# Two attention layers of a four-layer transformer trunk rewritten: masks without matmuls, transposes per key block, wider products

## The chip, the cores and the metric

The kernel runs on one core of a Trainium2 chip. The metric is the time of one execution on the device in microseconds; the profile is of one such execution. TensorE (PE) multiplies, VectorE (DVE), ScalarE (ACT) and GpSimd (POOL) do the rest, and SP and POOL also issue the DMAs.

## The reference

Input x is 512 rows of 1024 numbers in float32. Four residual layers follow each other, each with an RMS norm ahead: stick-breaking attention (16 heads of 64), a SwiGLU FFN (2816 wide), differential attention (8 heads, each with two maps of 64 and values of 128), and a second FFN.

```python
# stick-breaking, per head and block of 128 queries
earlier = key_pos[None, :] < q_pos[:, None]
log_keep = where(earlier, log_sigmoid(-z), 0.0)
log_after = cumsum(log_keep, reverse=True) - log_keep
weight = where(earlier, exp(log_sigmoid(z) + log_after), 0.0)
out = weight @ v
# differential: keys of the same or an earlier chunk of 64 are visible
q, k = rms_norm(q, q_g), rms_norm(k, k_g)     # per 64, then partial rotary
a = softmax(where(visible, q1 @ k1.T * scale, -1e30)) \
    - lam * softmax(where(visible, q2 @ k2.T * scale, -1e30))
o = rms_norm(a @ v, sub_g) * (1 - lam_init)
# FFN
x = x + (silu(h @ w_gate) * (h @ w_up)) @ w_down
```

## The kernel before

Activations lie transposed, as eight tiles of 128 features by 512 rows. Every float32 product is made of three matmuls of rounded halves (`mm3`, lines 203 to 205): high by high, high by low, low by high. Weights come in units of 128 x 1024. In the FFNs `wload` (L111 to L113) fetches a unit on SP's queue and splits it on ACT and DVE; in the attention layers `wload_dma` (L121 to L123) fetches it on POOL's queue into `whi`, ACT writes its negative into `wlo`, and a second DMA on POOL's queue adds the unit to that. Two sets of four buffers hold the halves.

An attention layer works pair by pair. In layer 0, q and k of a pair of heads are products of 512 columns (`ps_q`, `ps_k`), in layer 1 they are made for two heads at a time with 256 columns (`ps_nat`, `qk_chunk`, four `qk_nat` buffers), normalised per 64 columns and rotated there, the last two partly on POOL, and then transposed (`tqk`, L661). `stack_q` and `stack_k` lay the halves of q and k one above the other, so that one product of depth 128 gives two of the three terms: ACT and DVE write four pieces of 64 x 512, and two DMAs on POOL's queue copy k's into the other half (L278).

Scores (`scores`, L284 to L286) of one block of 128 queries are two products with a mask matmul between them, which adds -1e30 to the masked part of the diagonal block through an identity. Layer 0 takes two sigmoids of them, DVE runs a scan (L403) and DVE or, for every other block, POOL multiplies (L412). Layer 1 takes the maximum (L678), exps with their sums (L679), scales on POOL (L688) and combines on DVE (L692). A head is worked in two halves of two query blocks (`attend`), each with its transposes (`wt_group`, L296 to L304), the split into `wt_hi` and `wt_lo` (L306, L307) and value products of 256 columns into `av`. In layer 1 `head_out` then transposes the head's result (`tn`), takes its square sum, normalises (L731), transposes back (`tb`) and splits it (L743, L744). `out_proj` multiplies by the output weights (`ps_o`).

The pools of layer 1 hold eight PSUM banks of 512 columns: two for `ps_nat`, two for scores, one each for `tqk`, `tp`, `tn` and `av`. The program is written head by head, and a scheduler of the build sets the order on each engine from it by dependences and buffers; on the chip each engine then works in exactly that order. In the program of layer 1 the stacks of the next pair stand between the two halves of the odd head, and the q, k and v products of the next pair in the even and the odd head.

## Time and profile before

| | |
|---|---|
| median of 3 runs | 1323.24 us (1320.13 to 1327.58) |
| the profiled execution | 1320.52 us, span 1318.7 us |
| PE busy | 1258.5 us (95%), 6598 matmul records |
| DVE, ACT, POOL busy | 686.6, 539.5, 201.2 us |
| DMA | 149.16 MB |
| mean granted clock of PE | 0.985 |

Busy PE time is the time with at least one matmul under way; matmuls overlap, so the distance from start to start tells what one costs. Stages by the first and last matmul: layer 0 to 295.6 us, first FFN to 666.5, layer 1 to 954.5, second FFN to the end.

### The profile page before, as it was taken

How to read it: one execution, taken by the hardware profiler on the slowest of the kernel's cores; microseconds unless marked ns; L12 is line 12 of the kernel's file. 1: busy time of each engine (PE TensorE's matmuls, PEld its weight loads, DVE VectorE, ACT ScalarE, POOL GpSimd, SP SyncE). 2: the span in 40 equal slices, each digit the busy share in tenths (PEclk: the TensorE clock that was granted, in tenths of full speed). 3: DMA queues.
4: the chain of work that ended last, by engine and by line, in shares of the span. 5: the costliest groups of instructions: out<-in, count | busy, mean ns of one | idle time of the engine just before them, and what ended most of it. 6: DMA issues, size and time to landing. Idle time of an engine off the chain costs nothing.

```text
span 1318.7 us, 16917 instructions
## 1 busy us (share of the span) xinstructions
PE 1258.5 (95%) x6598; PEld 1066.8 (81%) x6598; DVE 686.6 (52%) x1250; ACT 539.5 (41%) x896; POOL 201.2 (15%) x283
## 2 busy tenths in 40 slices
PE   7999989889999999999989999988899999999998
PEld 5887878777888888888889999967688888888887
DVE  5465656655543344344533777875654434443442
ACT  5566655554331222122334666653443212221220
POOL 2233333310000000000015635531000000000000
PEclk9999999999999999999989999998999999999999
DMA  7656465353333333332368677553433333333222
GB/s 233 153 122 154 111 142 112 76 125 109 96 96 96 96 96 96 96 96 89 103 146 183 142 154 143 131 106 68 114 96 96 96 96 96 96 98 96 95 87 89
DMA packets 46159, 149.16 MB, mean 113 GB/s; under 512 B 6400, under 2 KB 6400, under 8 KB 46080
## 3 DMA queue, kind: packets, MB, share of 16 engines
q0 software_dynamic: 22464, 73.41, 25.7%
q1 hardware_dynamic: 23472, 74.67, 18.0%
q8 instruction: 52, 0.85, 0.3%
q14 instruction: 27, 0.22, 0.1%
q10 hardware_dynamic: 144, 0.01, 0.0%
HBM read 137.58 MB, written 2.10 MB: 106 GB/s over the span
## 4 chain that ended last, share of the span: by engine, by line
PE 74%; DMA 8%; issue 7%; DVE 5%; POOL 3%; ACT 2%; SPq 0%; POOLq 0%; DVEq 0%; ACTq 0%
PE ps_d L203 6%; PE ps_d L205 6%; PE ps_u L204 6%; PE ps_u L203 6%; PE ps_u L205 6%; PE ps_d L204 6%; PE ps_g L204 6%; PE ps_g L205 6%; PE ps_g L203 6%; PE ps_nat L203 2%; PE ps_nat L204 2%; PE ps_nat L205 2%; DMA whi<-in_wv 2%; DMA wlo<-in_wo 2%; DMA whi<-in_wqk 1%
## 5 line engine op out<-in xcount | busy, mean ns | idle before, releaser
L112 ACT ACTIVATE whi<-wraw 128x1024 fp32r<-128x1024 f32 (+1 forms) x138 | 142.7, 1037 | 475.1 <-PE ps_d L204 148.6
L113 DVE TENSOR_TENSOR wlo<-wraw,whi 128x1024 fp32r<-128x1024 f32 (+1 forms) x138 | 164.2, 1192 | 38.4 <-ACT whi L112 30.1
L204 PE MATMUL ps_nat<-wlo,hhi 128*128 128x256 f32 x512 | 148.3, 290 | 3.5 <-DMA wlo<-in_wqk 3.5
L203 PE MATMUL ps_nat<-whi,hhi 128*128 128x256 f32 x512 | 149.0, 291 | 2.6 <-issue 1.7
L205 PE MATMUL ps_nat<-whi,hlo 128*128 128x256 f32 x512 | 147.9, 289 | 0.0
L203 PE MATMUL ps_d<-ahi,whi 128*128 128x512 f32 x352 | 138.0, 394 | 0.0
L203 PE MATMUL ps_g<-hhi,whi 128*128 128x512 f32 x352 | 137.9, 392 | 0.0
L205 PE MATMUL ps_d<-ahi,wlo 128*128 128x512 f32 x352 | 137.7, 392 | 0.0
L205 PE MATMUL ps_g<-hhi,wlo 128*128 128x512 f32 x352 | 137.2, 390 | 0.0
L204 PE MATMUL ps_g<-hlo,whi 128*128 128x512 f32 x352 | 136.9, 390 | 0.0
L205 PE MATMUL ps_u<-hhi,wlo 128*128 128x512 f32 x352 | 136.9, 389 | 0.0
L204 PE MATMUL ps_u<-hlo,whi 128*128 128x512 f32 x352 | 136.9, 389 | 0.0
L203 PE MATMUL ps_u<-hhi,whi 128*128 128x512 f32 x352 | 136.9, 389 | 0.0
L204 PE MATMUL ps_d<-alo,whi 128*128 128x512 f32 x352 | 136.3, 388 | 0.0
L203 PEld LDWEIGHTS ps_nat<-whi,hhi 128*128 128x128 f32 x512 | 100.4, 196 | 4.6 <-issue 1.8
L204 PEld LDWEIGHTS ps_nat<-wlo,hhi 128*128 128x128 f32 x512 | 100.3, 196 | 4.6 <-DMA wlo<-in_wqk 4.2
L495 DVE TENSOR_TENSOR x<-x,ps_d 128x512 f32<-128x512 f32 x48 | 32.8, 687 | 132.5 <-PE ps_d L205 132.5
L205 PEld LDWEIGHTS ps_nat<-whi,hlo 128*128 128x128 f32 x512 | 100.2, 196 | 0.2
L483 DVE TENSOR_TENSOR u<-ps_u,rbc 128x512 f32<-128x512 f32 x44 | 30.4, 690 | 132.7 <-PE ps_u L205 132.7
L122 ACT ACTIVATE wlo<-whi 128x1024 fp32r<-128x1024 f32 x62 | 65.5, 1059 | 82.8 <-DMA whi<-in_wqk 29.0
L205 PEld LDWEIGHTS ps_d<-ahi,wlo 128*128 128x128 f32 x352 | 66.1, 188 | 15.4
L204 PEld LDWEIGHTS ps_d<-alo,whi 128*128 128x128 f32 x352 | 66.1, 188 | 14.8
(211 smaller groups left out, 2509.7 us busy)
## 6 DMA issues: line engine op xcount, KB each, us to landing
wraw<-in_wgu SPq DMA_DIRECT2D x88, 512.0 KB, 3.5
wraw<-in_wd SPq DMA_DIRECT2D x32, 512.0 KB, 3.5
whi<-in_wqk POOLq DMA_DIRECT2D x30, 512.0 KB, 4.1
wlo<-in_wqk POOLq DMA_DIRECT2D x30, 512.0 KB, 5.7
whi<-in_wv POOLq DMA_DIRECT2D x16, 512.0 KB, 5.8
wlo<-in_wv POOLq DMA_DIRECT2D x16, 512.0 KB, 5.7
k<-k POOLq DMA_DIRECT2D x32, 256.0 KB, 3.8
whi<-in_wo POOLq DMA_DIRECT2D x16, 512.0 KB, 4.5
```

The costliest lines, as they stand in the source:

```text
L112: A.activation(hi[:, :cols], raw[:, :cols], AF.Copy)
L113: eng.tensor_tensor(lo[:, :cols], raw[:, :cols], hi.bitcast(F32)[:, :cols], op=ALU.subtract)
L122: A.activation(lo, hi.bitcast(F32), AF.Copy, scale=-1.0)
L203: T.matmul(ps, lh[0], rh[0], start=first, stop=False)
L204: T.matmul(ps, lh[0], rh[1], start=False, stop=False)
L205: T.matmul(ps, lh[1], rh[0], start=False, stop=last)
L483: V.tensor_tensor(u32, pu, norm.bc, op=ALU.mult)
L495: V.tensor_tensor(x[m], x[m], ps, op=ALU.add)
```

## The change

The FFN code keeps its products; only their first four gate and up units per layer are loaded by `wload_dma`, and the unsplit units have a pool of three. Weights have five buffers for each half instead of four.

- Masks: no mask matmuls. In layer 0 the scan multiplies and adds an identity block (`delta`) from an initial 0, so that everything at and behind the diagonal becomes 0. In layer 1 DVE writes the masked corner of 64 x 64 of both maps into the scores.
- A head as a whole: blocks 3, 2, 1, 0 are weighed one after the other, the transposes are gathered by key block into banks for blocks (2, 3), (1) and (0), and the value products have 512, 384, 256 and 256 columns.
- Stacks: ACT and DVE write one pair of 128 x 512 halves (`hl`, one buffer), and eight DMAs on SP's queue lay them out: four for q, four for k.
- Layer 1: q and k of two heads come from one product of 512 columns, with two `qk_nat` buffers of twice the size; scores of both maps share one tile of two banks (one buffer); the gains are folded into the q stack and the rotation tables, which run on DVE; 1/s moves into `head_out`, whose squares come from four ACT instructions with accumulator. The stack transposes, `tn` and `tb` share one bank (`tq`). The stacks of the next pair follow `head_out` of the odd head.
- POOL issues DMAs only.

```diff
+WB = 5
...
+    def halves(pool, src, gain=None):
+        hl = pool.tile([P, 2, S], F32R, tag="hl", bufs=1, name="hl")
+        if gain is None:
+            A.activation(hl[:, 0], src, AF.Copy)
+            V.tensor_tensor(hl[:, 1], src, hl.bitcast(F32)[:, 0], op=ALU.subtract)
+        else:
+            A.activation(hl[:, 0], src, AF.Copy, scale=gain)
+            V.scalar_tensor_tensor(
+                hl[:, 1], src, gain, hl.bitcast(F32)[:, 0], op0=ALU.mult, op1=ALU.subtract
+            )
+        return hl
+
+    def stack_q(pool, src, gain=None):
+        hl = halves(pool, src, gain)
         q2 = pool.tile([P, 2, S], F32R, tag="q2", name="q2")
         for e in range(2):
             r = slice(e * 64, e * 64 + 64)
             o = slice(64 - e * 64, 128 - e * 64)
-            A.activation(q2[r, e], src[r], AF.Copy)
-            V.tensor_tensor(q2[o, e], src[r], q2.bitcast(F32)[r, e], op=ALU.subtract)
+            nc.sync.dma_start(out=q2.bitcast(F32)[r, e], in_=hl.bitcast(F32)[r, 0])
+            nc.sync.dma_start(out=q2.bitcast(F32)[o, e], in_=hl.bitcast(F32)[r, 1])
         return q2
 
-    def stack_k(pool, src):
+    def stack_k(pool, src, gain=None):
+        hl = halves(pool, src, gain)
         k2 = pool.tile([P, 2, 2, S], F32R, tag="k2", name="k2")
         for e in range(2):
             r = slice(e * 64, e * 64 + 64)
             o = slice(64 - e * 64, 128 - e * 64)
-            A.activation(k2[r, 0, e], src[r], AF.Copy)
-            V.tensor_tensor(
-                k2[r, 1, e], src[r], k2.bitcast(F32)[r, 0, e], op=ALU.subtract
-            )
-            G.dma_start(out=k2[o, :, e], in_=k2[r, :, e])
+            nc.sync.dma_start(out=k2.bitcast(F32)[r, :, e], in_=hl.bitcast(F32)[r])
+            nc.sync.dma_start(out=k2.bitcast(F32)[o, :, e], in_=hl.bitcast(F32)[r])
         return k2
...
+    def wt_bank(tpp, wts, w, kts):
+        tp = tpp.tile([P, S], F32, tag="tp", name="tp")
+        b = WOFF[kts[0]]
+        for kt in kts:
+            for qt in range(TT - 1, kt - 1, -1):
+                o = WOFF[kt] - b + (TT - 1 - qt) * P
+                T.transpose(tp[:, o : o + P], w[qt][:, kt * P : (kt + 1) * P], ident)
+        r = slice(b, WOFF[kts[-1] + 1])
+        n = r.stop - r.start
+        A.activation(wts[0][:, r], tp[:, :n], AF.Copy)
+        V.tensor_tensor(
+            wts[1][:, r], tp[:, :n], wts[0].bitcast(F32)[:, r], op=ALU.subtract
+        )
+
+    def wt_chunk(wts, kt):
+        n = S - kt * P if kt < 3 else 256
+        r = slice(WOFF[kt], WOFF[kt] + n)
+        return n, wts[0][:, r], wts[1][:, r]
+
+    def attend(tpp, wts, weigh):
+        w = [None] * TT
+        for qt in (3, 2):
+            w[qt] = weigh(qt)
+        wt_bank(tpp, wts, w, (2, 3))
+        w[1] = weigh(1)
+        wt_bank(tpp, wts, w, (1,))
+        w[0] = weigh(0)
+        wt_bank(tpp, wts, w, (0,))
...
-                scores(ps, q2, k2, e, qt, mask_sb)
+                scores(ps, q2, k2, e, qt)
...
-                    ones[:, 0:1].to_broadcast([P, n]),
-                    1.0,
+                    delta[:, S - n :][:, ::-1],
+                    0.0,
                     ALU.mult,
-                    ALU.mult,
-                )
-                eng = G if qt % 2 == 1 else V
-                eng.tensor_tensor(w[:, : n - 1], w[:, : n - 1], qq[:, 1:n], op=ALU.mult)
+                    ALU.add,
+                )
+                V.tensor_tensor(w[:, :n], w[:, :n], qq[:, 1:], op=ALU.mult)
...
-            qp = st.enter_context(tc.tile_pool(name="qp1", bufs=4))
+            qp = st.enter_context(tc.tile_pool(name="qp1", bufs=2))
...
-            scp = st.enter_context(tc.tile_pool(name="sc1", bufs=2, space=PSUM))
-            tpp = st.enter_context(tc.tile_pool(name="tp1", bufs=1, space=PSUM))
+            scp = st.enter_context(tc.tile_pool(name="sc1", bufs=1, space=PSUM))
+            tpp = st.enter_context(tc.tile_pool(name="tp1", bufs=2, space=PSUM))
+            tqp = st.enter_context(tc.tile_pool(name="tq1", bufs=1, space=PSUM))
...
+                gemm_nat([wqk1[c, j] for j in range(4)], h, evac, 512)
...
+                ps = scp.tile([P, 2, S], F32, tag="sc", name="sc")
+                for e in range(2):
+                    scores(ps[:, e], q2, k2, e, qt)
+                V.memset(ps[0:64, :, n - 64 : n], NEG)
+                V.reduce_max(nm, ps[:, :, :n], axis=AX.X, negate=True)
...
+            def head_out(av, ss):
+                ot = at.tile([P, S], F32, tag="ho", name="ot")
+                A.activation(ot, av, AF.Copy)
+                rs = sm.tile([P, TT], F32, tag="rs1", name="rs1")
+                V.reciprocal(rs, ss[:, 0])
+                tp = tqp.tile([P, S], F32, tag="tq", name="tn")
+                for t in range(TT):
+                    o = (TT - 1 - t) * P
+                    T.transpose(tp[:, t * P : (t + 1) * P], ot[:, o : o + P], ident)
+                v = sm.tile([P, 32], F32, tag="rs_v", name="o_ss")[:, :TT]
+                sq = tmp.tile([P, S], F32, tag="tmp", name="o_sq")
                 for t in range(TT):
                     c = slice(t * P, (t + 1) * P)
-                    T.transpose(tp[:, c], ot[:, c], ident)
-                on = at.tile([P, S], F32, tag="ho", bufs=2, name="on")
-                A.activation(on, tp, AF.Copy)
-                sq = ot
-                A.activation(sq, on, AF.Square)
-                v = sm.tile([P, 16], F32, tag="rs_v", name="o_ss")[:, :TT]
-                V.reduce_sum(v, sq.rearrange("p (t d) -> p t d", d=P), axis=AX.X)
+                    A.activation(
+                        sq[:, c],
+                        tp[:, c],
+                        AF.Square,
+                        scale=rs[:, t : t + 1],
+                        accum_out=v[:, t : t + 1],
+                    )
                 fin = sm.tile([P, TT], F32, tag="fin", name="fin")
                 V.tensor_scalar(fin, v, thr, None, op0=ALU.is_lt)
+                V.tensor_tensor(fin, fin, rs, op=ALU.mult)
                 V.tensor_scalar(v, v, 1.0 / P, eps_phi, op0=ALU.mult, op1=ALU.add)
                 u = rsqrt(v, TT)
                 V.tensor_tensor(u, u, fin, op=ALU.mult)
+                on = at.tile([P, S], F32, tag="ho", name="on")
                 V.tensor_tensor(
                     on.rearrange("p (t d) -> p t d", d=P),
-                    on.rearrange("p (t d) -> p t d", d=P),
+                    tp.rearrange("p (t d) -> p t d", d=P),
                     u.unsqueeze(2).to_broadcast([P, TT, P]),
                     op=ALU.mult,
                 )
-                tb = tpp.tile([P, S], F32, tag="tn", name="tb")
+                tb = tqp.tile([P, S], F32, tag="tq", name="tb")
...
+            qk = qk_chunk(0)
+            st_next = head_stacks(qk, 0)
             v = vn = v_chunk(0)
             og = []
             for hd in range(8):
                 hh = hd % 2
                 q2, k2 = st_next
                 if hh == 0:
-                    st_next = head_stacks(qn, kn, 1)
-                av = avp.tile([P, S], F32, tag="av", name="av")
-                attend(hh, 0, q2, k2, v, av)
+                    st_next = head_stacks(qk, 1)
+                av, ss = head(hh, q2, k2, v)
+                og.append(head_out(av, ss))
                 if hh == 0 and hd < 6:
-                    qn = qk_chunk(hd // 2 + 1, 0)
+                    qk = qk_chunk(hd // 2 + 1)
                 if hh == 1 and hd < 7:
-                    st_next = head_stacks(qn, kn, 0)
-                attend(hh, 1, q2, k2, v, av)
-                if hh == 1 and hd < 7:
+                    st_next = head_stacks(qk, 0)
                     vn = v_chunk(hd // 2 + 1)
-                if hh == 0 and hd < 6:
-                    kn = qk_chunk(hd // 2 + 1, 1)
-                og.append(head_out(av))
                 v = vn
```

The order on PE in layer 1, around the step from the third to the fourth pair of heads (the seventh head is the first of the fourth pair). `tqk` are the transposes for the next pair's stacks, `av` the odd head's value products, `ps_nat` the q, k and v products. Before:

```order
L205 MATMUL ps_nat_8161<-whi_8070,hlo_5227 128x256
L203 MATMUL ps_nat_8161<-whi_8070,hhi_5259 128x256
L204 MATMUL av_7924<-wt_lo0_5426,v1h_7290 128x256
L205 MATMUL av_7924<-wt_hi0_5425,v1l_7291 128x256
L203 MATMUL av_7924<-wt_hi0_5425,v1h_7290 128x256
L204 MATMUL av_7924<-wt_lo0_5426,v1h_7290 128x256
L205 MATMUL av_7924<-wt_hi0_5425,v1l_7291 128x256
L303 MATMUL tp_8043<-ident_91,e1_8003 128x128
L661 MATMUL tqk_7989<-ident_91,qk_nat_7739 128x128 x4
L204 MATMUL ps_nat_8161<-wlo_8071,hhi_5259 128x256
L205 MATMUL ps_nat_8161<-whi_8070,hlo_5260 128x256
L203 MATMUL ps_nat_8161<-whi_8075,hhi_5292 128x256
```

After the change, the same step (`sc` are the next pair's first scores):

```order
L743 MATMUL tn_7297<-ident_91,ot_7293 128x128 x4
L771 MATMUL tb_7327<-ident_91,on_7325 128x128 x4
L190 MATMUL ps_o_7788<-ohi_7332,whi_7819 128x512
L190 MATMUL ps_o_7842<-ohi_7332,whi_7873 128x512
L687 MATMUL tqk_7336<-ident_91,qk_nat_7034 128x128 x4
L191 MATMUL ps_o_7788<-olo_7333,whi_7819 128x512
L192 MATMUL ps_o_7788<-ohi_7332,wlo_7820 128x512
L191 MATMUL ps_o_7842<-olo_7333,whi_7873 128x512
L192 MATMUL ps_o_7842<-ohi_7332,wlo_7874 128x512
L687 MATMUL tqk_7349<-ident_91,qk_nat_7034 128x128 x4
L687 MATMUL tqk_7482<-ident_91,qk_nat_7034 128x128 x4
L285 MATMUL sc_7513<-k2_7357,q2_7344 128x512
```

Before, the transposes stood among the odd head's first value products, with `ps_nat` behind them; now `tn`, `tb`, the three `tqk` and the scores follow each other, with six `ps_o` products between them.

The order on POOL in layer 0, where the value weights of the second group of heads are fetched (`whi`, `wlo` are DMA issues, `w` the multiplication by the scan). Before:

```order
L121 DMA whi_862<-in_wv0 128x1024
L412 TENSOR_TENSOR w_522<-w_522,qq_525 128x511
L123 DMA wlo_863<-in_wv0 128x1024
L121 DMA whi_867<-in_wv0 128x1024
L412 TENSOR_TENSOR w_608<-w_608,qq_611 128x255
L123 DMA wlo_868<-in_wv0 128x1024
L412 TENSOR_TENSOR w_640<-w_640,qq_643 128x511
```

After the change, the same weights:

```order
L108 DMA whi_800<-in_wv0 128x1024
L110 DMA wlo_761<-in_wqk0 128x1024
L110 DMA wlo_801<-in_wv0 128x1024
L108 DMA whi_805<-in_wv0 128x1024
L110 DMA wlo_806<-in_wv0 128x1024
L108 DMA whi_1058<-in_wqk0 128x1024
L110 DMA wlo_1059<-in_wqk0 128x1024
```

The multiplications have left the queue; issues of `whi` and `wlo` follow each other.

## Rows read from the trace of the kernel before

**Rows 1.** The page: busy time and share of the span; the chain by engine.
```profile
PE 1258.5 (95%) x6598; PEld 1066.8 (81%) x6598; DVE 686.6 (52%) x1250; ACT 539.5 (41%) x896; POOL 201.2 (15%) x283
...
PE 74%; DMA 8%; issue 7%; DVE 5%; POOL 3%; ACT 2%; SPq 0%; POOLq 0%; DVEq 0%; ACTq 0%
```

**Rows 2.** Windows by stage; columns: length, busy of each engine, PEclk, DMA share, GB/s.
```profile
0.00:295.60 295.60, 263.39 (x1491) 222.24 (x1492) 173.19 (x329) 172.59 (x314) 87.71 (x115) 0.97 0.58 136
295.60:666.50 370.90, 367.84 (x1619) 303.03 (x1618) 170.28 (x220) 112.01 (x139) 3.36 (x5) 1.00 0.33 99
666.50:865.50 199.00, 193.01 (x1548) 186.04 (x1547) 132.62 (x371) 118.01 (x248) 92.78 (x139) 0.98 0.69 144
865.50:954.50 89.00, 73.94 (x362) 58.73 (x361) 54.50 (x138) 40.00 (x80) 17.31 (x25) 0.94 0.44 101
```

**Rows 3.** Timeline of PE in the second FFN: start, duration, line, operation, tiles.
```profile
1099.64 0.39 PE L203 MATMUL ps_g<-hhi,whi 128*128 128x512 f32 x1
...
1100.32 0.39 PE L203 MATMUL ps_g<-hhi,whi 128*128 128x512 f32 x1
```

**Rows 4.** Timeline of PE in the diff layer, two score tiles.
```profile
740.65 0.28 PE L284 MATMUL sc<-k,q 128*128 128x256 f32 x1
740.77 0.23 PE L285 MATMUL sc<-mask_ch,identb 128*128 128x128 bf16 x1
...
741.01 0.28 PE L284 MATMUL sc<-k,q 128*128 128x256 f32 x1
```

**Rows 5.** Waits of PE in layer 0: us in total, times, longest.
```profile
PE tp L304 <- POOL w L412: 9.1, 3, 3.5
```

**Rows 6.** The chain in layer 0: start, length, what.
```profile
56.76 6.34 DMA whi<-in_wv
```

**Rows 7.** Timeline of PE in layer 0, where two of the waits end.
```profile
63.49 0.40 PE L205 MATMUL ps_q<-hhi,wlo 128*128 128x512 f32 x1
...
179.15 0.48 PE L205 MATMUL ps_q<-hhi,wlo 128*128 128x512 f32 x1
```

**Rows 8.** Groups by form: line, operation, tiles, count | busy us, mean ns | idle before.
```profile
L307 DVE TENSOR_TENSOR wt_lo<-tp,wt_hi 128x384 fp32r<-128x384 f32 x48 | 26.4, 550 | 23.3 <-ACT wt_hi L306 23.3
...
L679 ACT ACTIVATION_READ_ACCUMULATOR e<-sc,nm 128x1 f32 x64 | 12.6, 196 | 0.0
...
L679 ACT ACTIVATE e<-sc,nm 128x512 f32<-128x512 f32 x16 | 11.0, 687 | 4.8 <-DVE nm L678 4.8
...
L678 DVE TENSOR_REDUCE nm<-sc 128x1 f32<-128x512 f32 x16 | 11.0, 685 | 1.5 <-PE sc L286 1.3
...
L622 DVE TENSOR_REDUCE qk_ss<-qk_sq 128x8 f32<-128x512 f32 x16 | 10.7, 681 | 18.2 <-ACT qk_sq L617 17.9
...
L412 DVE TENSOR_TENSOR w<-w,qq 128x383 f32<-128x383 f32 x16 | 10.3, 642 | 1.0
L632 DVE TENSOR_TENSOR qk_nat<-qk_nat,rs_u 128x1024 f32<-128x1024 f32 x8 | 10.2, 1281 | 0.2
...
L691 DVE TENSOR_TENSOR c<-c,nlam 128x1 f32<-128x1 f32 x32 | 7.6, 236 | 0.5
...
L679 ACT ACTIVATE e<-sc,nm 128x128 f32<-128x128 f32 x16 | 5.8, 363 | 9.3 <-DVE nm L678 6.1 <-DVE rs_u L135 3.0
```

**Rows 9.** Timeline of PE: the first score product of the diff layer.
```profile
719.35 0.28 PE L284 MATMUL sc<-k,q 128*128 128x256 f32 x1
```

**Rows 10.** Timeline of PE, then of DVE: head_out of the last head.
```profile
924.22 0.60 PE L719 MATMUL tn<-ident,ot 128*128 128x128 f32 x4
...
929.57 0.69 DVE L731 TENSOR_TENSOR on<-on,rs_u 128x512 f32<-128x512 f32 x1
```

**Rows 11.** DMA issues: queue, count, KB each, median us to landing.
```profile
k<-k POOLq DMA_DIRECT2D x32, 256.0 KB, 3.8
...
outT<-x SPq DMA_DIRECT2D x8, 256.0 KB, 2.0
```

**Rows 12.** Timeline of DVE in the diff layer: one of the 32 products of c.
```profile
735.80 1.10 DVE L691 TENSOR_TENSOR c<-c,nlam 128x1 f32<-128x1 f32 x1
```

362 lines of the change are left out of this document (162 added, 200 removed).

## The prediction

> **What bounds the kernel now.** I read the page's busy times and its chain first: TensorE (PE) is busy 95% of the span, and the chain that ended last is 74% PE [rows 1]. Then the busy times by stage [rows 2]: the FFN stretch is as good as full (367.8 of 370.9 us), the stick layer (layer 0) is not (263.4 of 295.6 us), and the diff layer (layer 1) is full while its q, k and v products last (193.0 of 199.0 us) and loose behind them (73.9 of 89.0 us). Then single matmuls: an FFN matmul of 512 columns starts every 0.2267 us (three in 0.68) [rows 3], a score product of 256 columns is followed by the next matmul 0.12 us later, and the three of one score tile (two products, one mask matmul) take 0.36 us, so the mask matmul takes 0.12 as well [rows 4]. So the FFNs (3168 matmuls x 0.2267 = 718 us of the span) are bound by PE and untouched; what can move are the two attention layers, and in them PE's work and PE's waits apart.
>
> **Terms of the sum.** The profiled run took 1320.5 us (span 1318.7); the median of the three runs, 1323.2, is 2.7 above it. I sum against 1320.5.
>
> *PE work removed.* 128 mask matmuls x 0.12 = 15.4 us, half in each layer. The value products go from twelve of 256 columns (1.44 us for one operand pair and head) to pieces of 512, 384, 256 and 256; 384 costs 0.173 by interpolating the two spacings, so a head falls from 1.44 to 1.28 in layer 0 (16 heads, 2.6 us) and from 2.16 to 1.92 in layer 1 (8 heads, 1.9 us). 768 products of 256 columns become 384 of 512: 92.2 - 87.1 = 5.1 us. Together 10.3 us in layer 0 and 14.7 in layer 1.
>
> *Layer 0.* Besides that work PE waits 9.1 us for POOL's multiplication of w, three times some 3 us [rows 5]: it stands in POOL's queue behind weight DMAs. The chain there goes through the issue of a `wlo` DMA and then 6.34 us of a weight DMA [rows 6]. The `ps_q` rows that end these waits lie at 63.49 and 179.15 [rows 7], two periods of four heads apart: 57.8 us each, in which PE has 50.3 us of work by counting the order. After, PE has 47.9, the waits on POOL are gone, and the multiplication costs VectorE some 0.6 to 0.8 us each (the 383-column one takes 0.64 [rows 8]) on an engine that is 59% busy in this stage [rows 2]. POOL's queue still alternates `whi` with a `wlo` that waits for ScalarE's negated copy, so I keep half of the gap: 51 us a period. Three periods save 20 us, the stretch around them (start, last heads) its 2.6 us of work and some 4 of stall: **-27 us**. Bounds: -45 if every stall goes, 0 if weights set the period.
>
> *Layer 1.* It takes 199.0 + 89.0 = 288 us now [rows 2]; the first scores start at 719.35 [rows 9], 53 us in. What decides the rest is what stands beside a head in PE's order. Before, `ps_nat` or `ps_o` products stand between nearly all steps of a head up to the end, and the stacks of the next pair are made between the two halves of the odd head. After, the products run ahead as far as two `qk_nat` buffers allow. PE's order then has 81.2 us of work from the first scores to those of the third head, 42.5 to the fifth, 17.4 to the seventh (2.7 of it `ps_o`). In those later pairs nothing hides the chain of a pair, and it is serial by its tiles: one score tile of two banks, one `tq` bank for the stack transposes and for both transposes of `head_out`, one `hl` buffer that the copies must have read before the next half is written.
>
> - Even head, 15 us. Per query tile: four score matmuls (0.9), corner memset (0.1), maximum over 2 x 512 columns (2 x 0.685 less one fixed part, 1.3), two exps with the read of the accumulator (2 x (0.687 + 0.196)) [rows 8]: 4.1 us, since the next scores need the one tile; 3.3, 2.6 and 2.1 for the shorter ones, 12.1; weights, transposes and copies behind the last, 3.
> - Odd head, 27 us, by VectorE. Its own maxima, combinations and `wt_lo` copies (two of 384 columns at 0.55, one of 512) are 9.1 us; `head_out` of the even head, 4.2 (small operations 2.7, `on` 0.69, `olo` 0.75); and the next pair's qk chunk, now of 2048 columns: four sums of 0.68, the product of 2 x 1.28 [rows 8], the rotation that was on POOL (eight operations, some 0.4 each, estimated from the 128-column to 384-column rows) and 1.6 of square root, 10.1. That is 23.4, with 3 to 4 us of waits.
> - Tail from the odd head's last weights to the next scores, 24 us. Transpose, copies and value products 3.7; `ot` 0.7; then `head_out`: in the row of the last head tn begins at 924.22 and `on` at 929.57 [rows 10], 5.35 us, in which copy, square and sum (0.60 + 0.63 + 0.69) become four squares with accumulator (4 x (0.363 + 0.196) = 2.2 [rows 8]): 5.7. `on`, tb, the ohi copy and olo 2.7; only then is `tq` free. q transposes 0.5, halves 1.5; k transposes and halves 1.9, which first wait about 2.5 us for the q copies to have been read; then the k copies, 3.8 us if they are like the `k<-k` copies now, 2.0 if like the `outT` rows [rows 11]. Semaphore hops make up the last 1 us.
>
> So a pair takes 15 + 27 + 24 = 66 us, against 52.1 and 49.6 us of PE work now that was nearly all used. Layer 1 is then 52 (lead-in) + 84 (81.2 and a few waits) + 66 + 66 + 31 (scores of the last two heads) + 45 (152 `ps_o` products x 0.2267 = 34.5, the last value products, and some 8 us waiting for the last `head_out`) = 344: **+56 us**. Bounds: -5, if chains hide everywhere and only the removed work is seen with what the last stage gives back; +80 with 75 us a pair.
>
> *The rest.* The eight copies per pair leave POOL's queue for SP's, which in the attention layers carries nothing else after the start; no weight waits behind them. The first four FFN weights by accumulating DMA, the larger weight pools and the new start order cost nothing as long as `ps_o` covers them (43 us of PE); without it, one weight DMA of 6.3 us each time. Setup gets some twenty small operations beside FFN products.
>
> VectorE waits for POOL today: a product of one column takes 0.236 us on average and once 1.10 us at 735.80 [rows 8, 12]. The Trainium skill (SBUF — State Buffer, "Who interferes with whom") says why: the two share one pair of ports under an exclusive lock, which a VectorE operation with two SBUF inputs can meet. The trace agrees in the spread. With POOL's arithmetic gone, 32 such products would give back 32 x 0.08 = 2.5 us of VectorE, and by the rule the sum would be some 3 us lower; I count none, as most lie off the chain.
>
> Sum: 1320.5 - 27 + 56 = **1350 us** (1349.5).
>
> **Rivals.** *The chain of a pair is shorter than I walk it* (the other side). Its place is the tail and the odd head of pairs 2 and 3. For it: today's heads overlap well though each has the same steps, my VectorE sum has 3 to 4 us of waits a pair, and one scores tile may turn round faster. Against it: PE's order has no product to put there. With 45 us a pair (-42), 24 for the last scores (-7) and 40 for the last stage (-5) the time is 1296; it decides at 52 us a pair, where losses and gains cancel.
> *Gains and losses cancel*: pairs of 52 us, 1321 us.
> *The stick layer gains only its work*, because the change does not do what it says for the weights: POOL issues only DMAs, but each `wlo` still waits in order for ScalarE, and the stacks add 1 MB a pair. Layer 0 gives 10 us or less, the total is 1367 to 1376. For it: weight DMAs are on the chain [rows 6]. Against: the DMA engines are busy 0.58 of this stage at 136 GB/s [rows 2]; 8 MB more on 40 MB make it about 0.7. The Trainium skill (DMA: Bandwidth & Descriptors, "Issuing engines are not separate DMA queues") has it that transfers issued by different engines interleave on the same 16 DMA engines, so that moving the copies to SP gives them no way of their own. No row here shows the two queues apart.
>
> **How the numbers follow.** A measurement of this kernel tells about 0.5% from no change. My forecast has 0.52 (its own range 1330 to 1364), the stick rival 0.13, the shorter chain 0.25 (1275 to 1312), cancelling 0.10. Slower is 0.52 + 0.13 = 0.65. The range of 8 in 10 reaches from 1288, which leaves out the better half of the shorter chain, to 1382, which holds the stick rival and most of the upper bound of a pair.
>
> **What would show it.** Right: PE idle 20 to 50 us in each of pairs 2 and 3 after the last `ps_nat`, ended by VectorE, ScalarE and the stack copies; the seventh head's scores over 60 us after the fifth's; no wait of `tp` for POOL in layer 0 and `ps_g` first near 268 us; FFN stretches unchanged. Wrong: `ps_nat` or `ps_o` filling these pairs, pairs below 52 us, or a layer 0 above 285 us.

## The result and the profile after

The changed kernel takes 1500.5 us (median of 4 runs, 1495.0 to 1502.6) against 1321.7 for the kernel before: a ratio of 1.134, with a 95% interval of 1.129 to 1.140. The forecast was 1350 us, range 1288 to 1382. The direction was right, the size a sixth of the loss: the sum added 29 us (-27 and +56) where 179 were lost. The profiled execution took 1495.0 us, with a span of 1493.3.

From the page of the changed kernel: PE's busy time, the granted clock by slice, and the chain by engine.

```profile
PE 1310.3 (88%) x5974; PEld 1074.8 (72%) x5974; DVE 663.5 (44%) x1268; ACT 518.9 (35%) x896; POOL 100.3 (7%) x146
...
PEclk9999989799999999999999986755699999999999
...
PE 60%; issue 21%; DMA 9%; POOL 3%; ACT 3%; DVE 2%; SPq 1%; POOLq 0%; ACTq 0%; DVEq 0%
```

PE has 9% fewer matmuls and is busy for longer than in [rows 1]; the chain is 60% PE instead of 74%, and 21% of it (7% before) is time in which the engine waited for nothing that the profile shows. The clock row shows one reason why busy time grew: in layer 1, where PE idles much, slices stand as low as 5 to 7 tenths of the clock.

The same windows as in [rows 2], with layer 1 cut at the first scores of the first, third, fifth and seventh head (columns as there):

```profile
0.00:329.80 329.80, 271.22 (x1386) 227.10 (x1387) 165.51 (x309) 162.10 (x297) 47.53 (x72) 0.92 0.66 155
329.80:696.30 366.50, 364.87 (x1595) 298.19 (x1594) 172.78 (x285) 113.39 (x141) 6.54 (x9) 1.00 0.33 100
696.30:760.90 64.60, 53.22 (x263) 45.48 (x261) 17.41 (x48) 18.39 (x25) 10.79 (x15) 0.89 0.67 145
760.90:872.30 111.40, 90.33 (x493) 78.06 (x493) 39.94 (x116) 42.99 (x94) 16.97 (x24) 0.92 0.65 147
872.30:963.30 91.00, 59.29 (x276) 47.92 (x277) 37.74 (x112) 31.54 (x80) 8.49 (x12) 0.74 0.45 104
963.30:1035.10 71.80, 38.44 (x121) 27.14 (x121) 36.08 (x108) 21.90 (x66) 0.00 (x0) 0.57 0.19 44
1035.10:1121.00 85.90, 66.36 (x253) 51.34 (x254) 40.01 (x102) 32.87 (x80) 9.09 (x13) 0.75 0.43 107
1121.00:1493.30 372.30, 366.54 (x1595) 299.56 (x1593) 154.09 (x193) 95.71 (x113) 0.86 (x1) 0.99 0.29 94
```

| stretch | before | forecast | after |
|---|---|---|---|
| layer 0 | 295.6 | 269 | 329.8 |
| first FFN | 370.9 | 371 | 366.5 |
| layer 1 | 288.0 | 344 | 424.7 |
| of it: to the first scores | 53 | 52 | 64.6 |
| first pair of heads | | 84 | 111.4 |
| second pair | | 66 | 91.0 |
| third pair | | 66 | 71.8 |
| rest | | 45 + 31 | 85.9 |
| second FFN and end | 364.2 | 364 | 372.3 |

(Layer 1 of the kernel before ends at 941.5 by its first second-FFN product and at 954.5 by its last `ps_o`, since the two overlap; after the change both lie at 1121. From 666.4 to 941.5 it is 275.1 us, and this figure is compared with the experiments.) That window before, for comparison:

```profile
666.40:941.50 275.10, 257.66 (x1875) 237.61 (x1874) 179.90 (x498) 153.99 (x323) 109.46 (x163) 0.98 0.61 130
```

So layer 0 lost 34 us where 27 were to be gained, and layer 1 lost 150 on that count. The walk of the third pair, the one with hardly any products beside it, was nearly right; the parts that were to be hidden were not.

Where PE's time in layer 1 went can be added up from the starts of its matmuls, each distance less what that shape takes at full clock. As an estimate, work comes to some 234 us (236 before), waits of over 0.4 us each to some 130 (19), and distances that are longer by less to some 56 (20). In the trace some 50 of these 56 us lie where the granted clock stood at its lower level (6 of the 20 before): most of them are work at half clock and not waits. Three of PE's four longest waits in layer 1 (total us, times, longest):

```profile
PE sc L285 <- DMA k<-hl: 20.0, 8, 4.2
...
PE tqk L687 <- DVE hl L254: 13.5, 3, 5.0
PE ps_nat L191 <- DMA wlo<-in_wv: 12.9, 4, 5.4
```

### The profile page after: what moved, and what is told of

Same layout as the page of the kernel before. It is cut to its first block, busy times and chain, and to the rows that moved or that the text cites. A ratio compares the mean times of both kernels' runs of the same rounds, so it can differ in the third digit from the quotient of the medians.

```text
span 1493.3 us, 15726 instructions
## 1 busy us (share of the span) xinstructions
PE 1310.3 (88%) x5974; PEld 1074.8 (72%) x5974; DVE 663.5 (44%) x1268; ACT 518.9 (35%) x896; POOL 100.3 (7%) x146
## 4 chain that ended last, share of the span: by engine, by line
PE 60%; issue 21%; DMA 9%; POOL 3%; ACT 3%; DVE 2%; SPq 1%; POOLq 0%; ACTq 0%; DVEq 0%
PE ps_u L192 5%; PE ps_u L191 5%; PE ps_u L190 5%; PE ps_d L192 5%; PE ps_d L191 5%; PE ps_d L190 5%; PE ps_g L192 5%; PE ps_g L190 5%; PE ps_g L191 5%; DMA k<-hl 2%; PE ps_nat L191 2%; DMA whi<-in_wqk 2%; PE ps_nat L190 2%; PE ps_nat L192 2%; POOL wlo L110 2%
## 5 line engine op out<-in xcount | busy, mean ns | idle before, releaser
L99 ACT ACTIVATE whi<-wraw 128x1024 fp32r<-128x1024 f32 (+1 forms) x128 | 132.5, 1037 | 449.8 <-PE ps_d L191 151.9
L100 DVE TENSOR_TENSOR wlo<-wraw,whi 128x1024 fp32r<-128x1024 f32 (+1 forms) x128 | 152.1, 1189 | 30.1 <-ACT whi L99 29.8
L191 PE MATMUL ps_nat<-wlo,hhi 128*128 128x256 f32 (+1 forms) x384 | 130.5, 340 | 13.9 <-DMA wlo<-in_wv 12.9
L190 PE MATMUL ps_nat<-whi,hhi 128*128 128x256 f32 (+1 forms) x384 | 130.8, 343 | 10.4 <-DVE v L364 3.9
L190 PE MATMUL ps_u<-hhi,whi 128*128 128x512 f32 x352 | 137.6, 391 | 0.0
L192 PE MATMUL ps_nat<-whi,hlo 128*128 128x256 f32 (+1 forms) x384 | 129.3, 337 | 0.0
L285 PE MATMUL sc<-k,q 128*128 128x256 f32 (+2 forms) x128 | 55.2, 434 | 70.0 <-DMA k<-hl 32.6
L191 PEld LDWEIGHTS ps_nat<-wlo,hhi 128*128 128x128 f32 x384 | 79.6, 207 | 20.3 <-DMA wlo<-in_wv 13.8
L190 PEld LDWEIGHTS ps_nat<-whi,hhi 128*128 128x128 f32 x384 | 78.9, 206 | 18.8 <-DVE v L364 4.7
L285 PEld LDWEIGHTS sc<-k,q 128*128 128x128 f32 x128 | 30.3, 237 | 82.7 <-issue 37.7
L192 PEld LDWEIGHTS ps_nat<-whi,hlo 128*128 128x128 f32 x384 | 79.4, 207 | 5.4
```

Of the source, the lines that this page charges most:

```text
L99: A.activation(hi[:, :cols], raw[:, :cols], AF.Copy)
L100: V.tensor_tensor(lo[:, :cols], raw[:, :cols], hi.bitcast(F32)[:, :cols], op=ALU.subtract)
L190: T.matmul(ps, lh[0], rh[0], start=first, stop=False)
L191: T.matmul(ps, lh[0], rh[1], start=False, stop=False)
L192: T.matmul(ps, lh[1], rh[0], start=False, stop=last)
L285: T.matmul(ps[:, :n], q2[:, e, qs], k2[:, 0, e, :n], start=True, stop=False)
```

## The experiments

In all of them layer 0 is counted to the first product of the first FFN and layer 1 from the last `ps_d` to the first product of the second. Where only one run was made its single time stands. The order that the build chooses differs from kernel to kernel as well, and it alone can move a stage: layer 0, with the same code, took 329.8 us in the changed kernel and 335.3 with early stacks, and two of the kernels below with the same code in layer 1 differ by 9.6 us there. So a difference of less than some 10 us in one run is not told apart from that.

### Weights: the loop of two DMAs and a copy

In layer 0 of the changed kernel the engines and their queues wait, among others, as follows (who, for what, total us, times, longest):

```profile
POOL wlo L110 <- ACT wlo L109: 159.6, 25, 15.3
...
ACT wlo L109 <- DMA whi<-in_wqk: 37.9, 10, 6.8
...
PE sc L285 <- ACT w L414: 16.1, 5, 5.5
...
PE sc L285 <- DMA k<-hl: 12.6, 5, 4.7
```

POOL, which has only DMAs left, waits 160 us for ScalarE's negated copies, and ScalarE for the units to land. ScalarE works in order, so what stands behind such a copy waits too. Its timeline at one place, and PE's at the same place:

```profile
126.19 0.48 ACT L413 ACTIVATE keep<-sc,rn 128x256 f32<-128x256 f32 x1 [0.88 <-DVE qq L416]
130.49 1.06 ACT L109 ACTIVATE wlo<-whi 128x1024 fp32r<-128x1024 f32 x1 [3.81 <-DMA whi<-in_wqk]
131.45 1.51 ACT L414 ACTIVATE w<-sc,rp 128x512 f32<-128x512 f32 x3
```

```profile
127.34 0.39 PE L192 MATMUL ps_q<-hhi,wlo 128*128 128x512 f32 x1
132.17 0.58 PE L285 MATMUL sc<-k,q 128*128 128x256 f32 x1 [4.44 <-ACT w L414]
```

ScalarE is free at 126.7, but the next instruction in its order is the copy of a unit that is still on its way; it runs at 130.49, the sigmoid `w` at 131.45, and only then are score tiles free for PE, which had stopped after 127.34. Theory A of the runs below is that this loop (a unit by DMA, the copy, a second DMA, all in order on two queues) sets the pace.

**Low halves without the loop.**

```diff
...
-        A.activation(lo, hi.bitcast(F32), AF.Copy, scale=-1.0)
-        G.dma_start(out=lo, in_=ap, accum_op=ALU.add)
+        G.dma_start(out=lo, in_=ap)
```

> The changed kernel with the low halves of the attention weights loaded by a plain DMA, without ScalarE's negated copy and without the wait for it (the low half then holds the whole weight, so one of the three terms of each product is left out of the right value; the matmuls are the same). Theory A (the loop of weight DMA, ScalarE copy, second DMA on POOL's queue sets the pace of layer 0): layer 0 falls from 330 us to 270 to 285, layer 1 by 10 to 20, in all some 1425 to 1445. Theory B (the stack copies through hl set it): layer 0 moves by less than 10 us, in all above 1480.

Measured: 1437.2 us. The windows of layer 0 and layer 1:

```profile
0.00:307.80 307.80, 263.98 (x1387) 220.09 (x1388) 164.50 (x308) 131.98 (x265) 36.82 (x74) 0.97 0.61 169
676.60:1066.90 390.30, 289.69 (x1403) 235.26 (x1402) 169.07 (x484) 116.02 (x314) 33.86 (x64) 0.82 0.42 124
```

Layer 0 fell by 22.0 us and its mean clock rose from 0.92 to 0.97; layer 1 fell by 34.4, more than expected. The kernel moves as many bytes as before this edit (170.1 MB), so what was gained is the loop and ScalarE's copy and not traffic. The loop is a cause in both layers, though layer 0 missed the expected 285.

**q and k weights of layer 0 once, on SP's queue:**

```diff
...
-                gemm_t(ps, wload_dma(wqk0[p]), h)
+                gemm_t(ps, wload(rq, wqk0[p]), h)
```

(and the same for k, with two raw buffers.)

> The changed kernel with the q and k weights of layer 0 fetched once on SP's queue and split by ScalarE and VectorE (as in the FFN), so that POOL's queue there holds the value and output weights alone; all values as in the reference. Theory A (the loop of two DMAs and a copy per unit on one queue): layer 0 falls from 330 to 295 to 308, as with the direct low halves. If DMA traffic or the stacks set its pace, it falls by less than 10.

Measured: 1471.7 us. Layer 0:

```profile
0.00:313.20 313.20, 270.45 (x1387) 224.00 (x1388) 183.64 (x334) 164.50 (x300) 27.58 (x45) 0.94 0.57 140
```

16.6 us less, 5 short of the expected band. ScalarE still makes a copy of each unit here, so its work alone is not what the loop cost; q and k alone carry most of the effect.

### The stacks: copies through one buffer

**Stacks made as before**: ScalarE and VectorE write 64-row pieces, k is completed by two copies on POOL's queue.

```diff
...
-        hl = halves(pool, src, gain)
...
-            nc.sync.dma_start(out=k2.bitcast(F32)[r, :, e], in_=hl.bitcast(F32)[r])
-            nc.sync.dma_start(out=k2.bitcast(F32)[o, :, e], in_=hl.bitcast(F32)[r])
+            A.activation(k2[r, 0, e], src[r], AF.Copy)
...
+            G.dma_start(out=k2[o, :, e], in_=k2[r, :, e])
```

> The changed kernel with the stacks made as before: ScalarE and VectorE write 64-row pieces, two k copies on POOL's queue, no hl. Theory B (stack copies): the three steps between pairs in layer 1 lose the q copies and one wait each, 8 to 12 us, and with the clock layer 1 falls from 424 us by 35 to 60; layer 0 by some 15. In all 1430 to 1450. Theory A (weights): less than 15 us in all, or slower, since the k copies stand in POOL's queue again.

Measured: 1449.3 us. Both layers:

```profile
0.00:304.90 304.90, 265.81 (x1387) 222.82 (x1387) 176.63 (x323) 171.16 (x313) 57.48 (x88) 0.96 0.61 139
673.80:1077.40 403.60, 301.66 (x1403) 246.52 (x1402) 182.21 (x502) 157.98 (x361) 55.22 (x80) 0.80 0.44 97
```

Layer 0 gave 24.9 us (15 expected), layer 1 only 21.1 (35 to 60 expected). So the copies cost layer 0 as much as the loop of weights did. (The edit takes out the eight copies, 17 MB of transfers and the one buffer `hl` together; which of them counts is not separated.)

**Both edits together.**

> The edits of the direct low halves and of the stacks as before, together. If A and B are separate causes the gains add, to some 1370 to 1390, with layer 0 at 255 to 270 us; if both touch the same wait, the sum is clearly less than that of the two alone.

Measured: 1409.5 us; layer 0 283.7, layer 1 384.5. Both are outside what was expected (1370 to 1390 in all, layer 0 at 255 to 270). In layer 0 the two add all the same (46.1 against 22.0 + 24.9), so they are separate causes. Without them layer 0 is 11.9 us shorter than in the kernel before, which still has its own loop; the kernel before without that loop took 278.9 us there (below). In layer 1 they overlap (40.2 against 34.4 + 21.1), and 384 us is still 109 above the kernel before.

### The place of the stacks

The step between the third and fourth pair in the changed kernel, PE's timeline (start, duration, tiles, what ended the idle time before it) and SP's issues at the same place:

```profile
1007.94 0.47 PE L303 MATMUL tp<-ident,e 128*128 128x128 f32 x1 [3.69 <-DVE e L714]
...
1013.98 0.66 PE L743 MATMUL tn<-ident,ot 128*128 128x128 f32 x4 [0.69 <-ACT ot L737]
1019.82 1.08 PE L771 MATMUL tb<-ident,on 128*128 128x128 f32 x4 [5.18 <-DVE on L762]
...
1022.70 1.05 PE L687 MATMUL tqk<-ident,qk_nat 128*128 128x128 f32 x4
...
1025.32 1.12 PE L687 MATMUL tqk<-ident,qk_nat 128*128 128x128 f32 x4
1030.23 1.12 PE L687 MATMUL tqk<-ident,qk_nat 128*128 128x128 f32 x4 [3.79 <-DVE hl L254]
1035.09 0.76 PE L285 MATMUL sc<-k,q 128*128 128x512 f32 x1 [3.74 <-DMA k<-hl]
```

```profile
1024.51 1.12 SPq L268 DMA_DIRECT2D q<-hl  x2
1025.73 1.19 SPq L269 DMA_DIRECT2D q<-hl  x2
1030.20 0.62 SPq L278 DMA_DIRECT2D k<-hl  x1
```

From the odd head's last weights (1007.94) to the next scores (1035.09) 27.2 us pass; the walk had 24. In it `tn` to `tb` takes 5.84 us, the second `tqk` waits for the bank, the third for the halves of k, which could be written to `hl` only when the q copies had read it (3.79 us), and the scores for the k copies. SP issues each copy for some 0.6 us, four in a row, before the last can land.

**Next stacks ahead of the head**, two `tq` banks and one `tp` bank:

```diff
...
+                if hh == 0 and hd < 6:
+                    qk_next = qk_chunk(hd // 2 + 1)
+                if hh == 1 and hd < 7:
+                    qk = qk_next
+                    st_next = head_stacks(qk, 0)
                 av, ss = head(hh, q2, k2, v)
                 og.append(head_out(av, ss))
...
```

> The changed kernel with the next pair's q and k products and stacks written ahead of the head instead of behind its head_out, and two banks for tq, one for tp. If the place of the stacks in the order of layer 1 makes the chain (theory C), pairs 1 and 2 fall from 91 and 72 us to some 60 and 50 and layer 1 by 40 to 60. If VectorE and the single score tile make it, layer 1 falls by less than 15 us. Layer 0 is unchanged (330 us).

Measured: 1447.1 us. Layer 1:

```profile
704.20:1075.10 370.90, 280.93 (x1403) 231.63 (x1402) 169.61 (x486) 147.25 (x347) 46.15 (x65) 0.88 0.56 129
```

53.8 us less, the largest single effect in layer 1, and the mean clock rose from 0.78 to 0.88. The place is a cause, as theory C has it. The edit moves the next pair's products and one bank together with the stacks, and what each is worth is not separated.

**Early stacks, made as before.**

> The changed kernel with the next pair's stacks written ahead of the head (two tq banks, one tp) and made as before (64-row pieces, two k copies on POOL's queue). If place and copies are separate parts of the chain between pairs, layer 1 falls from 424 us by 54 + 21, to some 350, layer 0 to 305, in all 1390. If early stacks already hide the copies, layer 1 stays at 365 to 371, in all 1405 to 1415.

Measured: 1383.2 us. Layer 1:

```profile
672.70:1011.30 338.60, 274.56 (x1402) 228.61 (x1401) 181.80 (x501) 156.56 (x362) 55.74 (x81) 0.89 0.52 116
```

86.1 us less, 11 more than the sum of the two (53.8 + 21.1).

**And low halves without the loop.**

> The same with the low halves of the attention weights loaded by a plain DMA (the low half holds the whole weight, as before). If weights, copies and place are the whole cause, both attention layers come near their PE work with the kernel before's stalls: layer 0 near 284, layer 1 275 to 300, in all 1300 to 1330. If a fourth cause remains in layer 1 (one score tile for both maps, VectorE's work, value products only behind the whole head), layer 1 stays above 320.

Measured: 1346.2 us; layer 0 284.4, layer 1 324.0. The three causes hold 100.7 of the 149.6 us in layer 1. A remainder of 49 us is left.

### The remainder in layer 1

These start from early stacks made as before (338.6 us in layer 1). Each undoes one more piece of the change. All are single runs, and the kernel before took 1323 to 1329 us (medians) beside them.

**A score tile for each map.**

```diff
...
-                ps = scp.tile([P, 2, S], F32, tag="sc", name="sc")
-                for e in range(2):
-                    scores(ps[:, e], q2, k2, e, qt)
-                V.memset(ps[0:64, :, n - 64 : n], NEG)
-                V.reduce_max(nm, ps[:, :, :n], axis=AX.X, negate=True)
                 for e, o in ((0, e1), (1, e2)):
+                    ps = scp.tile([P, S], F32, tag="sc", name="sc")
+                    scores(ps, q2, k2, e, qt)
+                    V.memset(ps[0:64, n - 64 : n], NEG)
+                    V.reduce_max(nm[:, e : e + 1], ps[:, :n], axis=AX.X, negate=True)
...
```

> The changed kernel with early stacks made as before (339 us in layer 1), and the scores of the two maps in two tiles of one bank, each with its own memset and maximum, instead of one tile of two banks. If the single tile makes the waits of the scores for the exps (19 us in the run of all three edits), layer 1 falls by 12 to 25 us, to 315 to 327. If VectorE's work or the value products behind the whole head make them, it falls by less than 5, or grows by the 32 extra maxima and memsets.

Measured: 1382.8 us, layer 1 338.6: no change. PE's waits for the exps are still there: 15.9 us in 16 waits, where the run without the edit had 16.0 us in 8.

**Heads in two halves** (the transposes and value products of the kernel before):

> The changed kernel with early stacks made as before, and each head of layer 1 worked in two halves again, with the transposes and the 256-column value products of the kernel before. If the whole head (all weights first, all value products behind) makes what is left, layer 1 falls from 339 us to 300 to 315; if the merged q and k chunk makes it, less than 8 us, or some us more for the 5 us of added PE work and the four more copies.

Measured: 1387.5 us, layer 1 347.9: 9.3 us more. By itself this piece gives nothing back.

**q and k by two products of 256 columns**, two weight units each:

> The changed kernel with early stacks made as before, and q and k of two heads from two products of 256 columns with two weight units each, as before, into the same tile. PE gets 5 us more work. If a chunk of four weight units holds the products up (the loop of units on POOL's queue), layer 1 falls from 339 us by 10 to 25; if the head's form makes what is left, it stays within 8 us or grows by 5.

Measured: 1374.8 us, layer 1 330.4: 8.2 less, in spite of 5 us more of PE work, and below the 10 to 25 expected. The width gained nothing that can be seen here; that a chunk of four units cost more fits, but 8 us in one run do not show it.

**From that, the products behind the even head's value products:**

> The changed kernel with early stacks made as before and 256-wide chunks (330 us in layer 1), the next pair's q and k products written behind the even head's value products instead of ahead of the even head. The order of PE then has 25 us of products left at the fourth head and 3 at the fifth, as against 25 and 0. If the products are used up too early for the late heads, layer 1 falls by no more than these 3 to 8 us; by the order alone they cannot be kept for the last four heads.

Measured: 1365.8 us, layer 1 323.0: 7.4 less, within what was expected of the order, but no more than builds differ by.

**256-wide chunks, half heads and two score tiles together:**

> The changed kernel with early stacks made as before, 256-wide chunks, heads in two halves and a score tile for each map: of the change in layer 1 only VectorE's work (corner memsets, the rotation and the combination without POOL), head_out with its squares and the shared tq banks are left. If the single tile and the whole head act only together, layer 1 falls from 330 to 285 to 305; if VectorE's added work and head_out make the rest, it stays at 318 to 340.

Measured: 1362.2 us. Layer 1:

```profile
673.70:990.70 317.00, 274.16 (x1835) 251.66 (x1834) 184.29 (x566) 162.12 (x378) 55.90 (x81) 0.91 0.58 125
```

13.4 less than with the chunks alone, where half heads and two tiles alone gave nothing: if they act, they act only together and weakly. 317 us lies 12 above the band of that theory and 1 below the band of the other, that VectorE's work and `head_out` make the rest. That these do was not tried by itself and stays open, with 42 us in it. What the trace shows is that four heads still had their `tn` to come when the last `ps_nat` was done, against three before.

### Parts of the change in the kernel before

**Scan as mask in layer 0**, no mask matmuls there, all multiplications on VectorE:

```diff
...
-                eng = G if qt % 2 == 1 else V
-                eng.tensor_tensor(w[:, : n - 1], w[:, : n - 1], qq[:, 1:n], op=ALU.mult)
+                V.tensor_tensor(w[:, :n], w[:, :n], qq[:, 1:], op=ALU.mult)
```

> The kernel before with one part of the change in layer 0: no mask matmuls, the scan with delta, the multiplication of w on VectorE for all blocks. The forecast's terms for these: 7.7 us of PE work and 9 us of waits for POOL, so layer 0 from 296 to 279 to 288 and 1304 to 1313 in all. If the gap between POOL's operations was set by weights all along (what the direct low halves say of the changed kernel), it gains 0 to 8 us only.

Measured: ratio 1.0054 (1.0028 to 1.0080); layer 0 297.8. Neither the 7.7 us of PE work nor the 9.1 us of waits came off the time. The waits stayed, under another name:

```profile
PE tp L305 <- DVE w L421: 18.2, 6, 5.0
```

[Rows 5] named POOL. ScalarE's timeline in this run, and then the same place in the kernel before:

```profile
65.08 1.06 ACT L122 ACTIVATE wlo<-whi 128x1024 fp32r<-128x1024 f32 x1 [4.13 <-DMA whi<-in_wv]
66.04 0.67 ACT L410 ACTIVATE keep<-sc,rn 128x512 f32<-128x512 f32 x1
66.61 0.68 ACT L411 ACTIVATE w<-sc,rp 128x512 f32<-128x512 f32 x1
```

```profile
63.12 1.06 ACT L122 ACTIVATE wlo<-whi 128x1024 fp32r<-128x1024 f32 x1 [4.07 <-DMA whi<-in_wv]
64.08 0.67 ACT L400 ACTIVATE keep<-sc,rn 128x512 f32<-128x512 f32 x1
64.65 0.68 ACT L401 ACTIVATE w<-sc,rp 128x512 f32<-128x512 f32 x1
```

At this one of the six places, as in the kernel before, ScalarE stands four us before a `wlo` copy until the unit has landed, and the two sigmoids behind it come late, then the scan, then the multiplication, by whichever engine. The wait was named after its last link.

**No mask matmuls in layer 1 too**, with 64 memsets on VectorE:

> The same, and in layer 1 too no mask matmuls: VectorE writes the masked corner of 64 x 64 into each score tile (64 memsets of some 0.15 us). PE loses 7.7 us of work in layer 1, VectorE gets some 10. While products hide the heads layer 1 falls by 4 to 7 us; if VectorE's part of a head is what its end waits for, it grows by up to 10.

Measured: ratio 1.0127 (1.0086 to 1.0168); layer 1 285.2 against 275.8 in the scan-mask run. That looks like the price of VectorE's additions, but the trace does not say so. Up to the transposes `tn` of the sixth head the two runs are level (216.1 and 216.8 us into the layer), so up to there the memsets cost no more than the mask matmuls gave. The loss arises in the last two heads. There PE waits 5.5 us for the last `on`, since the build put six `ps_o` products ahead of it instead of some twenty. The second line below is from the run of the scan mask on top of weights on SP's queue, further down, which leaves layer 1 as in the kernel before and has the same wait:

```profile
943.35 1.09 PE L750 MATMUL tb<-ident,on 128*128 128x128 f32 x4 [5.50 <-DVE on L741]
```

```profile
921.58 1.09 PE L749 MATMUL tb<-ident,on 128*128 128x128 f32 x4 [5.52 <-DVE on L740]
```

So that order comes without the memsets too, and what these cost by themselves stays open.

**q and k weights of layer 0 on SP's queue:**

```diff
...
-                gemm_t(ps, wload_dma(wqk0[p]), h)
+                gemm_t(ps, wload(wqk0[p]), h)
```

> The kernel before with the q and k weights of layer 0 fetched once on SP's queue and split by ScalarE and VectorE. If the waits that the profile of before puts down to POOL's multiplication come from the weight loop, layer 0 falls from 296 to 275 to 288, and the total to 1300 to 1315. If they come from POOL's arithmetic, less than 5 us.

Measured: ratio 0.989 (0.986 to 0.992); layer 0 285.1.

**Value weights too:**

> The same with the value weights of layer 0 too. Two raw buffers then carry all of its units; VectorE gets 8 more subtractions of 1.2 us. By the weight loop another 2 to 8 us less than with q and k alone; if the two raw buffers or VectorE become the limit, the same or up to 5 us more.

Measured: ratio 0.986 (0.983 to 0.988); layer 0 278.9. The wait of `tp` for POOL, with POOL's arithmetic left as it was, has gone from 9.1 us to:

```profile
PE tp L304 <- POOL w L412: 1.4, 1, 1.4
```

So the loop of weights cost layer 0 of the kernel before 16.7 us as well. (These units are read once instead of twice, so the kernel also moves 137.6 MB instead of 149.2; loop and traffic are not separated here, as they are in the changed kernel.)

**Scan as mask on top of that:**

> The kernel before with layer 0's q, k and v weights on SP's queue, and in layer 0 the scan as mask, no mask matmuls, all multiplications of w on VectorE. With the weight loop gone the 7.7 us of PE work should now count: layer 0 from 279 to 270 to 275. If VectorE (16 more multiplications of 0.8 us and the 24 subtractions) or ScalarE has become what the heads wait for, 0 or some us more.

Measured: ratio 0.994 (0.992 to 0.996); layer 0 280.0, 1.1 us more than without. PE's wait for the multiplication is now 2.2 us, where it was 18.2 in the scan-mask run with the loop, and the removed mask matmuls do not pay even so. (Layer 1 took 286.9 against 277.3 with the same code there: the two are level up to the sixth head, 216.9 and 218.2 us, and the loss lies in the order of the last two, as shown above.)

**Output weights too, in both layers:**

```diff
...
-            ws[g, 0] = wload_dma(wo[layer, 0, g])
+            ws[g, 0] = wload(wo[layer, 0, g])
...
```

> The kernel before with layer 0's q, k and v weights and both layers' output weights fetched once on SP's queue. PE waits 4.6 us (layer 0) and 7.6 us (layer 1) for low halves of output weights now; by the weight loop these go: 3 to 10 us below the run with q, k and v alone. VectorE gets 16 more subtractions of 1.2 us beside the last heads; if they come into the heads' chains, the same or up to 5 us more.

Measured: 1290.1 us, ratio 0.972 (0.969 to 0.975): the fastest version, 2.8% below the kernel before. Its page, and the windows of layers 0 and 1:

```profile
PE 1247.0 (97%) x6598; PEld 1061.8 (82%) x6598; DVE 730.3 (57%) x1288; ACT 540.0 (42%) x896; POOL 144.9 (11%) x207
```

```profile
0.00:277.50 277.50, 259.20 (x1514) 220.87 (x1515) 210.13 (x346) 174.46 (x318) 41.32 (x55) 0.99 0.31 91
639.70:921.50 281.80, 263.22 (x1899) 244.08 (x1898) 191.02 (x513) 158.90 (x328) 100.18 (x147) 0.97 0.54 117
```

PE is busy 97% of the span, and the clock hardly falls. The gain over the run with the q, k and v weights is 18 us by the medians, where 3 to 10 were expected. It lies at the ends of both layers, where `ps_o` no longer waits for low halves (4.6 and 7.3 us in that run): the first FFN takes 362.2 us from its first product to its last instead of 369.0, and layer 1 281.9 to its last `ps_o` instead of 290.6.

## Why the prediction was wrong

**The FFNs.** "Bound by PE and untouched": 366.5 and 372.3 us by the windows, against 370.9 and 364.2. Right within the way in which the ends overlap.

**Layer 0, the step that failed.** The prediction said that PE "waits 9.1 us for POOL's multiplication of w" which "stands in POOL's queue behind weight DMAs", that these waits are gone after the change, and kept half of the gap: -27 us, at worst 0. The scan run shows the wait staying when POOL's arithmetic is out of it, and the runs with weights on SP's queue show it going when only the weight loads are changed. The link that set it was ScalarE's wait, in order, for a unit, further up the same chain: the 6.34 us of DMA stand in [rows 6]. The change left that loop as it was. A second step failed beside it: the sum put the copies of the stacks at nothing ("no weight waits behind them"), and layer 0 fell by 24.9 us without them. Of the two they are the one that is new in layer 0, since the loop cost 16.7 us in the kernel before as well. Beside them the loop got slower too (the median from issue to landing of the q and k units' first DMA rose from 4.1 to 6.0 us), and the score tiles wait for both. The rival "the stick layer gains only its work" named the loop, but its price stopped at 0.

**Layer 1, the step that was mis-sized.** The mechanism was right: the stacks behind `head_out`, one bank, one `hl`. By itself the place is worth 54 us, with the copies 86. The walk of a pair with few products beside it was near: in the third pair the even head took 17.4 us for 15, the odd head 27.2 for 27, the tail 27.2 for 24. What failed is what the sum did with the other pairs. "81.2 and a few waits" took the tail of the first pair to be hidden by products: 111.4 instead of 84, of which PE's waits for halves, copies and value weights are 16. The second pair was priced at the bare chain although 42.5 us of PE work were to run in it, against 17.4 in the third: 91.0 instead of 66. The lead-in was left at its old length: 64.6 instead of 52. The loop of weights has a part in this, since with the direct low halves the first scores came 6.5 us earlier and the `tn` of the second head 23 us earlier.

**What the sum did not have.** Every wait and every product was priced at full clock. Layer 1 ran at a mean clock of 0.78, the third pair at 0.57: between the two levels of 1.2 and 2.4 GHz a mean of 0.78 means some 43% of the time, 184 us, at the lower one, against 14 us before. Some 50 of the 56 us of slow distances lie there. By this estimate the clock accounts for some 44 us more than before, over half of the 81 us by which layer 1 missed its 344. It fell with the waits and rose with each edit that took most of them out, and no run changes it alone.

**The signs.** PE idled 31.7 and 33.4 us in the second and third pairs (window less busy time), and the seventh head's scores came 71.8 us after the fifth's, as the prediction asked of a right walk. Its sign of being wrong, a layer 0 above 285 us, came too.

**The parts counted as gains.** The -7.7 us of mask matmuls in each layer did not show when tried alone: layer 0 took 2 us more, and layer 1 was level up to the sixth head. Of the 5 us of wider products nothing could be seen either. In these runs PE work that was taken out where PE waits for another engine came back as wait.

**The rivals.** The shorter chain had 0.25 and was refuted by every pair. The rule of the Trainium skill on the pair of ports that VectorE and POOL share (SBUF — State Buffer, "Who interferes with whom") agrees with the trace: without POOL's arithmetic the multiplication of 384 columns takes 0.549 us in the mean where one of 383 took 0.642 [rows 8]. Of the sixteen before, the five that took 0.73 us or more all ran while POOL multiplied; the others took at most 0.56.

```profile
L424 DVE TENSOR_TENSOR w<-w,qq 128x384 f32<-128x384 f32 x16 | 8.8, 549 | 0.7 <-ACT w L414 0.5
```

For these sixteen that is 1.5 us of VectorE, and no time was gained by it; the prediction had counted none.

## What to carry to other kernels

Before a wait is priced by the engine that ended it, follow its chain two links further up and ask what stood in front in that engine's in-order queue; the cheapest test is to move the suspected link to another queue and see whether the wait stays under a new name. A loop of DMA, copy and second DMA on two in-order queues is paid twice, since everything behind the copy waits for the first transfer as well; one load on its own queue for most attention weights was worth 2.8% here. A chain that loses its cover should be priced with the clock that PE gets when it idles, and each moved piece separately, since here the place, the copies and the loop of weights were each worth over 20 us of layer 1. A stage that grows after an edit should be compared head by head before the edit is blamed: in one run here the loss of 9 us lay in the order at the end.

## What was not expected of the hardware

The granted clock fell in long stretches, not only at stalls: in layer 1 it came to 0.89, 0.92, 0.74, 0.57 and 0.75 in the five windows above, and rose with the edits that took most of the waits out (0.78, 0.88, 0.89 and 0.91 for layer 1 of the changed kernel, of early stacks, of early stacks made as before, and of 256-wide chunks with halves and two tiles). From 1017.4 to 1061.8 us it stood at the lower level throughout, although PE was busy for 24.4 us of these 44.4. PE's timeline where it returns to full speed:

```profile
879.34 0.63 PE L190 MATMUL ps_nat<-whi,hhi 128*128 128x512 f32 x1
879.77 0.63 PE L191 MATMUL ps_nat<-wlo,hhi 128*128 128x512 f32 x1
...
881.45 0.39 PE L190 MATMUL ps_nat<-whi,hhi 128*128 128x512 f32 x1
881.68 0.39 PE L191 MATMUL ps_nat<-wlo,hhi 128*128 128x512 f32 x1
```

Products of 512 columns start 0.43 us apart in the first two rows and 0.23 apart in the last two. Ahead of this stretch PE had waited 4.7 us for the halves of k and 3.8 us for its copies; from 877.9 us on these products follow each other without a wait.
